# Modulation vectors from TensorE in four 32-column groups, in a hybrid Fourier / RG-LRU / PEER layer

## The chip, the core and the metric

The kernel runs on one core of a Trainium2 chip. The metric is the device time of one launch in microseconds (us). Engines are named as in the profile: PE (TensorE matmul) and PEld (its weight loads), DVE (VectorE), ACT (ScalarE), POOL (GpSimd) and SP (SyncE, which here only issues DMAs).

## The reference

One layer over 512 latent tokens and 256 context tokens of width 1024. Two conditioning vectors, `c` for the latents and `c_ctx` for the context, become six modulation vectors of 1024 each:

```
mod_x = silu(c) @ w_mod + b_mod        # w_mod: 1024 x 6144, fp32, 25 MB
mod_c = silu(c_ctx) @ w_mod + b_mod
sh1, sc1, g1, sh2, sc2, g2 = split(mod, 6)
hx = rmsnorm(x, norm1_g) * (1 + sc1_x) + sh1_x
hc = rmsnorm(ctx, norm1_g) * (1 + sc1_c) + sh1_c
f, u, g = split(h @ w_in, ...)                       # 512 columns each
...                                                  # Fourier group of f; conv, gates and scans of u; gelu(g)
x = x + g1_x * (concat(rmsnorm(fourier), rmsnorm(rec)) @ w_out)
h2 = rmsnorm(x, norm2_g) * (1 + sc2_x) + sh2_x
x = x + g2_x * peer_ffn(h2)                          # product keys, 16384 experts
return rmsnorm(x, final_norm_g)
```

The context needs only the first two of its six vectors, since only its recurrences' last states are used.

## The kernel before

Channels lie on the 128 partitions: x is eight tiles `x2[d]` of 128 x 512, the context eight of 128 x 256, and a modulation vector is eight columns of the tile `mods` (128 x 48) or, for the context, of `modc` (128 x 16: columns 0 to 7 are sh1, 8 to 15 are sc1). Matmuls of full precision are made of three passes in a rounded fp32 form (`mm3`, lines 128 to 130: high x high, high x low, low x high), so each weight tile is split into a high part (ACT copy, `whi`) and a low part (subtraction, `wlo`, line 119, on DVE unless POOL is named). The few matmuls in plain fp32 show as two PE rows each.

The work up to about 300 us is written out by hand; `in_order` pins PE, ACT and DVE to the order of the program text. DMAs on the SP queue follow the pool's buffers: a weight tile of 1 MB (`load`, tile `raw`) can be fetched only when one of the two buffers of its tag is free. The stages, with the lines by which they can be found:

- Start: x, ctx and the first part of `w_mod` are loaded. The sc1 columns are row products: `w_mod` arrives transposed (one output column per partition, 1024 inputs along it), and `mod_dot` (line 229) multiplies a 128 x 1024 block by silu(c), broadcast to all partitions, and sums it on DVE; for the context POOL multiplies (line 239) and ACT sums. The sh1 vectors are matmuls instead (`shift_mm`, line 258: two stationary columns, 512 moving ones, plain fp32), turned into columns by eight tiny matmuls (`shift_cols`, line 264).
- `norm1` multiplies by the reciprocal root mean square on DVE and POOL; `make_hx` scales and shifts on ACT, rounds on ACT, and takes the low part on DVE.
- The projections of u (`u_mm`, `u_block`), convolutions (lines 391 to 395), gates (`gates`), gate branches (`gate_branch`), decays, scans (lines 448 to 455).
- The Fourier projection `f_mm`, the DFT over positions (`dft_seq`) and over head channels (`dft_head`).
- The output projection: eight rounds of `out_mm` (24 passes each), `out_add` (lines 678, 681), the next weights, `rec_norm`; then the sums of squares of the new x (`x2_sums`), their reciprocal root, and `h2` (lines 755 to 757).
- PEER, from about 299 us to the end.

The columns 16 to 47 of `mods` (g1, sh2, sc2, g2) are made by `mod_cols(w)`: it loads 1 MB of `w_mod` and makes two dots of 128 x 1024 on DVE. These calls stand between the steps above: four among gates, branches and scans, three in the Fourier projection, two in the DFT of the heads (as four `mod_col`), and seven in the output projection, one after each round but the last. g1 is needed from the first `out_add`; sh2 and sc2 at `h2`; g2 in PEER.

## Time and profile before

| | |
|---|---|
| median of 3 runs | 1640.66 us (1638.37 to 1642.04) |
| the profiled execution, own time | 1642.68 us |
| its span in the trace | 1640.8 us |
| PE busy, whole span | 1480.7 us (90%) |
| DVE busy, whole span | 1320.9 us (81%) |
| ACT, POOL busy | 641.8 us, 586.1 us |
| granted PE clock, mean | 0.962 of full speed |

How to read it: the part up to 299 us is where the change lies. In the table by stages a row gives the length of a stretch, then the busy time of each engine in it with the number of instructions, the granted PE clock, the DMA engines' busy share and the data rate. In a list in order of time a row gives start, duration, engine, line, operation, tiles and shapes, the count of instructions run together, and in brackets how long the engine sat idle before it and what released it.

### The profile page before, as it was taken

The numbers are of one execution on the slowest core, as the hardware profiler recorded it, in microseconds if no ns is written. First come the engines' busy times: TensorE is split into PE (matmuls) and PEld (weight loads), VectorE is DVE, ScalarE is ACT, GpSimd is POOL, SyncE is SP. The second block draws the span as 40 slices with busy tenths as digits, with TensorE's granted clock in tenths as the row PEclk, the third lists the DMA queues.
The fourth block names the chain that finished last, engine by engine and source line by source line (L and its number), as shares of the span: only waits on it lengthen the run. The fifth ranks groups of instructions, "written<-read, shape, count | busy, mean of one in ns | idle before, by whom it ended". The sixth has DMA issues, their size and how long they took to land.

```text
span 1640.8 us, 22365 instructions
## 1 busy us (share of the span) xinstructions
PE 1480.7 (90%) x8423; PEld 1383.7 (84%) x8423; DVE 1320.9 (81%) x2366; ACT 641.8 (39%) x957; POOL 586.1 (36%) x415
## 2 busy tenths in 40 slices
PE   2896886799989999999899998999999999889986
PEld 0484664588869999999899998999999999889986
DVE  7689989699988996676778787778777778789973
ACT  4656641433334555333242332323323232224342
POOL 6325356466430000323333533334343334322312
PEclk9997898899999999999999999999999999999998
DMA  9223535223216998986879787788878788899831
GB/s 345 99 77 113 181 120 227 92 87 103 94 71 232 295 307 267 360 327 221 314 263 335 284 308 297 261 328 287 320 276 317 275 301 308 294 352 336 301 109 44
DMA packets 125393, 390.92 MB, mean 238 GB/s; under 512 B 9060, under 2 KB 62436, under 8 KB 101988
## 3 DMA queue, kind: packets, MB, share of 16 engines
q1 hardware_dynamic: 88132, 254.93, 43.2%
q0 software_dynamic: 37152, 134.56, 23.0%
q8 instruction: 66, 1.08, 0.3%
q14 instruction: 43, 0.35, 0.1%
HBM read 354.33 MB, written 35.13 MB: 237 GB/s over the span
## 4 chain that ended last, share of the span: by engine, by line
PE 42%; DVE 15%; DMA 14%; issue 12%; POOL 5%; ACT 2%; DVEq 0%; POOLq 0%; SPq 0%; ACTq 0%
PE ps_ps L129 8%; PE ps_ps L128 8%; PE ps_ps L130 8%; DMA row<-vrow,eidx 6%; DMA row<-urow,eidx 6%; PE ps_pa L128 5%; PE ps_pa L130 5%; PE ps_pa L129 5%; POOL row L1068 4%; DVE wlo L119 3%; DVE oacc L1090 1%; PE ps_ps L980 1%; PE ps_ps L981 1%; DVE junk L229 1%; DVE row L1074 1%
## 5 line engine op out<-in xcount | busy, mean ns | idle before, releaser
L66 ACT ACTIVATE whi<-raw 128x1024 fp32r<-128x1024 f32 x296 | 312.7, 1059 | 734.4 <-PE ps_ps L129 398.2
L128 PE MATMUL ps_pa<-h2h,whi 128*128 128x384 f32 x1024 | 354.5, 346 | 15.2 <-ACT act L66 15.2
L129 PE MATMUL ps_ps<-wl,whi 128*128 128x384 f32 x1024 | 349.0, 341 | 7.9 <-DVE wl L119 7.9
L130 PE MATMUL ps_ps<-wh,wlo 128*128 128x384 f32 x1024 | 349.2, 341 | 7.5 <-DVE wlo L119 7.5
L130 PE MATMUL ps_pa<-h2h,wlo 128*128 128x384 f32 x1024 | 350.8, 343 | 5.4 <-DVE wlo L119 5.4
L128 PE MATMUL ps_ps<-wh,whi 128*128 128x384 f32 x1024 | 349.1, 341 | 4.4 <-ACT wh L66 4.1
L129 PE MATMUL ps_pa<-h2l,whi 128*128 128x384 f32 x1024 | 351.6, 343 | 0.0
L119 DVE TENSOR_TENSOR wlo<-raw,whi 128x1024 fp32r<-128x1024 f32 x263 | 325.4, 1239 | 31.8 <-ACT whi L66 29.1
L1068 POOL DMA_INDIRECT row<-urow,eidx x128 | 163.4, 1277 | 447.1 <-DVE row L1074 238.5
L1068 POOL DMA_INDIRECT row<-vrow,eidx x128 | 167.9, 1312 | 292.2 <-DVE oacc L1090 216.6
L1074 DVE SCALAR_TENSOR_TENSOR row<-row,hrow 128x1024 f32<-128x1024 f32 x128 | 155.1, 1221 | 92.2 <-DMA row<-urow,eidx 91.9
L1090 DVE SCALAR_TENSOR_TENSOR oacc<-row,gw,oacc 128x1024 f32<-128x1024 f32 x127 | 162.5, 1279 | 70.9 <-DMA row<-vrow,eidx 70.7
L128 PEld LDWEIGHTS ps_pa<-h2h,whi 128*128 128x128 f32 x1024 | 196.1, 191 | 17.8 <-ACT act L66 16.5
L130 PEld LDWEIGHTS ps_ps<-wh,wlo 128*128 128x128 f32 x1024 | 194.9, 190 | 9.4 <-DVE wlo L119 9.3
L129 PEld LDWEIGHTS ps_ps<-wl,whi 128*128 128x128 f32 x1024 | 194.8, 190 | 8.7 <-DVE wl L119 8.7
L130 PEld LDWEIGHTS ps_pa<-h2h,wlo 128*128 128x128 f32 x1024 | 195.4, 191 | 7.1 <-DVE wlo L119 6.7
L128 PEld LDWEIGHTS ps_ps<-wh,whi 128*128 128x128 f32 x1024 | 194.9, 190 | 4.9 <-ACT wh L66 4.4
L129 PEld LDWEIGHTS ps_pa<-h2l,whi 128*128 128x128 f32 x1024 | 196.0, 191 | 0.5
L119 POOL TENSOR_TENSOR wlo<-raw,whi 128x1024 fp32r<-128x1024 f32 x33 | 80.7, 2446 | 103.2 <-ACT whi L66 70.2
L1039 DVE SCALAR_TENSOR_TENSOR x<-ps_ps,mods,x 128x384 f32<-128x384 f32 x128 | 78.3, 611 | 31.0 <-PE ps_ps L130 30.7
L1014 DVE TENSOR_TENSOR act<-act,gt 128x384 f32<-128x384 f32 x128 | 67.7, 551 | 11.1 <-DMA gt<-Gd 10.1
L66 ACT ACTIVATE wh<-act 128x384 fp32r<-128x384 f32 x128 | 62.7, 518 | 24.1 <-DVE act L1014 21.8
(280 smaller groups left out, 2137.5 us busy)
## 6 DMA issues: line engine op xcount, KB each, us to landing
raw<-u SPq DMA_DIRECT2D x64, 1024.0 KB
raw<-v SPq DMA_DIRECT2D x64, 1024.0 KB
Gd<-stg SPq DMA_DIRECT2D x24, 1024.0 KB
gt<-Gd SPq DMA_DIRECT2D x16, 1536.0 KB
raw<-wm SPq DMA_DIRECT2D x18, 1024.0 KB
raw<-wq SPq DMA_DIRECT2D x8, 1024.0 KB
Ad<-act SPq DMA_DIRECT2D x10, 768.0 KB
act<-Ad SPq DMA_DIRECT2D x10, 768.0 KB
```

Of the source, the lines that this page charges most:

```text
L66: return S.activation(o, i, f, **kw)
L119: lo_ins[0] = (lo_eng or V).tensor_tensor(dst[1], src, dst[0].bitcast(F32), op=ALU.subtract).ins
L128: PE.matmul(ps, a[0], b[0], start=start, stop=False)
L129: PE.matmul(ps, a[0], b[1], start=False, stop=False)
L130: PE.matmul(ps, a[1], b[0], start=False, stop=stop)
L229: return V.scalar_tensor_tensor(junk, wt, 1.0, sil[z], op0=ALU.mult, op1=ALU.mult, accum_out=dst).ins
L980: PE.matmul(o, X0[:, k, :, r], Y1[:, k, :, r], start=True, stop=False)
L1014: V.tensor_tensor(av, av, self.gt[:, :, j], op=ALU.mult)
L1039: V.scalar_tensor_tensor(xd, ps[:, :TD], mods[:, 40 + d:41 + d], xd, op0=ALU.mult, op1=ALU.add)
L1068: G.indirect_dma_start(out=t[:TG], out_offset=None, in_=tab, in_offset=bass.IndirectOffsetOnAxis(ap=eidx[:TG, s:s + 1], axis=0))
L1074: ins = V.scalar_tensor_tensor(t, t, 1.0, hrow[:TG], op0=ALU.mult, op1=ALU.mult, accum_out=dots[:TG, s:s + 1])
L1090: ins = V.scalar_tensor_tensor(o, t, gw[:TG, s:s + 1], o, op0=ALU.mult, op1=ALU.add)
```

## The change

All 48 columns of `mods` and 16 of `modc` come from PE. `w_mod` is kept in natural layout and loaded as 24 tiles of 128 inputs x 2048 outputs (`mod_load(n)`, n = 8m + d: m is the third of the outputs, d the eighth of the inputs). The stationary operand `cc32[:, d]` is 128 x 32: silu(c), silu(c_ctx) and thirty columns of zeros. `mod_mm(n)` makes four plain fp32 matmuls of 512 moving columns; number j writes PSUM partitions 32j to 32j+31, so each uses another 32-column group of the array, and a third is summed over its eight loads in one PSUM bank (`pm`). `mod_out(m)` copies the bank to SBUF on ACT, turns it with four matmuls against a selection matrix (four columns for each vector), and adds the bias on DVE.

```diff
+    cc32 = cpool.tile([P, ND, 32], F32, name="cc32")
+    V.memset(cc32, 0.0)
-    (loads of two broadcast c vectors, of sc1 blocks 0 to 3, of 16 shift tiles; x and ctx between them)
+    def mod_load(n, st=""):
+        rawm[n] = load(wm[n // 8, n % 8], st)
+    for d in range(ND):
+        nc.sync.dma_start(x2[d], xT[d])
+    for n in range(4):
+        mod_load(n, ("", "U")[n % 2])
+    for d in range(ND):
+        nc.sync.dma_start(xn[d][:, :C], ctxT[d])
+    for n in range(4, 8):
+        mod_load(n, ("", "U")[n % 2])
     rawu = {0: load(wu[0], cuts=2)}
...
-    def mod_dot(dst, wt, z): ...      # DVE row product with sum
-    def sc_dots(w): ...               # two dots, two POOL products
-    def shift_mm(n, ds): ...
+    def mod_mm(n):
+        m, d = n // 8, n % 8
+        if d == 0:
+            modp[m] = pst("pm")
+        t = rawm.pop(n)
+        for j in range(4):
+            PE.matmul(modp[m][32 * j:32 * j + 32], cc32[:, d], t[:, j * 512:(j + 1) * 512],
+                      start=(d == 0), stop=(d == ND - 1))
+    def mod_out(m):
+        sb = bt(F32, 512)
+        act(sb, modp[m], AF.Copy)
+        pT = pst("pa", 32)
+        for b in range(4):
+            PE.matmul(pT[:, 8 * b:8 * b + 8], sb[:, b * P:(b + 1) * P], vec[:, V_SEL:V_SEL + 8], start=True, stop=True)
+        ...                             # one bias add into mods, for m = 0 one into modc
...
+    mean_squares(x2, T, ssx, range(ND))
+    for n in range(3):
+        mod_mm(n)
     mean_squares([xn[d][:, sc] for d in range(ND)], C, ssc, range(ND))
+    for n in range(3, 8):
+        mod_mm(n)
+    mod_out(0)
-    (norm1 on DVE and POOL; make_hx: two scale-and-shift and a rounding on ACT, one subtraction on DVE)
+    def hx_norm(d):
+        hx.append(bt2(L))
+        for z, src, sl, mm in ((1, xn[d][:, sc], sc, modc), (0, x2[d], sx, mods)):
+            V.scalar_tensor_tensor(xn[d][:, sl], src, A1[:, z, d:d + 1], rstd[:, sl], op0=ALU.mult, op1=ALU.mult)
+            act(hx[d][0][:, sl], xn[d][:, sl], AF.Identity, bias=mm[:, d:d + 1])
+    def hx_low(d):                      # two DVE operations, 256 and 512 wide
...
     def mod_cols(w, st=""):
-        mod_col(2 * w, st)
-        mod_col(2 * w + 1, st)
+        mod_load(8 + w, st)
+        if w:
+            mod_mm(7 + w)
+        if w == 8:
+            mod_out(1)
...
-    ss2 = pst("pa")                     # and ssf = pst("pm")
+    ss2 = []                            # both taken from "pa" where they are used
...
-    rsqrt(rstd2, bt(F32, 512), ss2, 1024)
-    mod_bias(24, 48)
+    rsqrt(rstd2, bt(F32, 512), ss2[0], 1024)
+    mod_mm(23)
+    mod_out(2)
```

The low part of the second half of the first weights moves from POOL to DVE. The loads of columns 16 to 47 stand where they stood, as many MB, but a block is multiplied one `mod_cols` call later than it is loaded.

On PE at the very start (L282 and L241 are the sums of squares, L258 the shift matmuls, L211 the four-group matmuls, L264 and L219 the turning ones), the rows up to the first projection:

```order
-L282 MATMUL ps_ps<-b,ones 128x512 x4
-L258 MATMUL ps_pa<-b,cc 2x512 x4
-L282 MATMUL ps_ps<-b,ones 128x256 x8
-L258 MATMUL ps_pa<-b,cc 2x512 x4
-L264 MATMUL ps_pm<-i_101,b 128x2 x4
-L258 MATMUL ps_pa<-b,cc 2x512 x4
+L1211 UNCONDITIONAL_BRANCH
+L241 MATMUL ps_ps<-b,ones 128x512 x4
+L211 MATMUL ps_pm<-raw,cc_98 32x512 x12
+L241 MATMUL ps_ps<-b,ones 128x256 x8
+L211 MATMUL ps_pm<-raw,cc_98 32x512 x20
+L219 MATMUL ps_pa<-vec,b 128x8 x4
```

Eight blocks (32 matmuls) now stand ahead of the first projection, split by the context's sums of squares.

On PE between the gates of the last two channel blocks and the last gate branch:

```order
 L129 MATMUL ps_ps<-b,whi 128x512
 L130 MATMUL ps_ps<-b,wlo 128x512
+L211 MATMUL ps_pm<-raw,cc_98 32x512 x12
 L128 MATMUL ps_pa<-b,whi 128x512
 L129 MATMUL ps_pa<-b,whi 128x512
```

Three blocks in a row are put in there; the first frees the buffer of the next Fourier weights.

On DVE in the rounds of the output projection, before (L229 is a dot, L681 an `out_add`, L119 a low part, L609 a `rec_norm` split) and then after (L622, L119 and L552 are the same three):

```order
L229 SCALAR_TENSOR_TENSOR junk,mods<-raw,sil 128x1024 x2
L681 SCALAR_TENSOR_TENSOR b<-ps_ps,mods,b 128x512 x2
L119 TENSOR_TENSOR wlo<-raw,whi 128x1024
L609 SCALAR_TENSOR_TENSOR b<-b,vec 128x512 x2
L229 SCALAR_TENSOR_TENSOR junk,mods<-raw,sil 128x1024 x2
L681 SCALAR_TENSOR_TENSOR b<-ps_ps,mods,b 128x512 x2
```

```order
L622 SCALAR_TENSOR_TENSOR b<-ps_ps,mods,b 128x512 x2
L119 TENSOR_TENSOR wlo<-raw,whi 128x1024
L552 SCALAR_TENSOR_TENSOR b<-b,vec 128x512 x2
L622 SCALAR_TENSOR_TENSOR b<-ps_ps,mods,b 128x512 x2
```

The two dots between rounds are gone from DVE; on PE one block stands after each round's 24 passes instead.

More of the change, by code (lines that the diff above doesn't have):

```diff
@@ L218, in build @@
     tact(sg, cc, AF.Sigmoid)
-    V.tensor_tensor(cc, cc, sg, op=ALU.mult)
-    for z in range(2):
-        for q in range(2):
-            sg = bt(F32, 512)
-            o = sil[z][:, q * 512:(q + 1) * 512]
-            tact(sg, o, AF.Sigmoid)
-            V.tensor_tensor(o, o, sg, op=ALU.mult)
-    def mod_dot(dst, wt, z):
-        junk = p1c.tile([P, 1024], mybir.dt.bfloat16, tag="junk", name="junk")
-        return V.scalar_tensor_tensor(junk, wt, 1.0, sil[z], op0=ALU.mult, op1=ALU.mult, accum_out=dst).ins
@@ L231, in mod_bias @@
-    def mod_bias(a, b):
-        V.tensor_tensor(mods[:, a:b], mods[:, a:b], vec[:, V_BMOD + a:V_BMOD + b], op=ALU.add)
-    def sc_dots(w):
-        for k in (2 * w, 2 * w + 1):
-            mod_dot(mods[:, 8 + k:9 + k], wsc[k], 0)
-            tag = ("whi", "wlo")[k % 2]
-            pr = wspl.tile([P, 1024], F32, tag=tag, name=tag)
-            G.tensor_tensor(pr, wsc[k], sil[1], op=ALU.mult)
-            prods.append((pr, modc[:, 8 + k:9 + k]))
-    prods = []
-    def sc_sums(n):
-        for _ in range(n):
-            pr, dst = prods.pop(0)
-            act(pr, pr, AF.Copy, accum_out=dst)
@@ L250, in build @@
-    shp = [pst("pa"), pst("pa")]
-    shr = [bt(F32, 512), bt(F32, 512)]
-    shT = pst("pm", 16)
-    shv = shT.rearrange("p (d z) -> p z d", z=2)
-    hx = []
-    def shift_mm(n, ds):
-        for d in ds:
-            PE.matmul(shp[n][:2], cc[:, d, :], wsh[d, n], start=(d == 0), stop=(d == ND - 1))
-        if d == ND - 1:
-            act(shr[n][:2], shp[n][:2], AF.Copy)
-    def shift_cols(n):
-        for d in range(4 * n, 4 * n + 4):
-            PE.matmul(shT[:, 2 * d:2 * d + 2], shr[n][:2, d % 4 * P:(d % 4 + 1) * P], i2, start=True, stop=True)
-        sl = slice(4 * n, 4 * n + 4)
-        for z, mm in enumerate((mods, modc)):
-            V.tensor_tensor(mm[:, sl], shv[:, z, sl], vec[:, V_BMOD + 4 * n:V_BMOD + 4 * n + 4], op=ALU.add)
+    V.tensor_tensor(cc32[:, :, 0:2], cc, sg, op=ALU.mult)
@@ L323, in build @@
+    def hx_low(d):
+        for sl, mm in ((sc, modc), (sx, mods)):
+            V.scalar_tensor_tensor(hx[d][1][:, sl], xn[d][:, sl], mm[:, d:d + 1], hx[d][0][:, sl].bitcast(F32),
+                                   op0=ALU.add, op1=ALU.subtract)
     pss0 = [(pst(), pst()) for h in range(2)]
@@ L359, in build @@
     decay = decay_rates()
-    for d in range(4, ND):
-        make_hx(d)
+    for d in range(3, ND):
+        hx_norm(d)
+        hx_low(d - 1)
         next(decay, None)
-    for d in range(2, ND):
-        u_mm(pss0, wpu, d)
+        u_mm(pss0, wpu, d - 1)
+    hx_low(ND - 1)
+    u_mm(pss0, wpu, ND - 1)
+    for _ in decay:
+        pass
     wpu1 = [split_w(rawu[1], h, V, "U") for h in range(2)]
```

123 lines of the change are left out of this document (32 added, 91 removed).

## The prediction

> **What bounds the kernel now.** The change ends at about 299 us, so I first cut the span into the stages of the program and read the busy times of each (length, then PE, PEld, DVE, ACT, POOL, the granted PE clock, DMA share, GB/s):
>
> ```profile
> 0.00:41.00 41.00, 8.20 (x10) 2.35 (x11) 29.31 (x23) 16.57 (x27) 27.64 (x15) 1.00 0.96 345
> 61.20:89.40 28.20, 27.75 (x130) 20.32 (x131) 15.26 (x40) 20.63 (x30) 2.39 (x1) 0.89 0.14 44
> 89.40:134.60 45.20, 39.57 (x200) 32.80 (x198) 37.24 (x52) 28.60 (x42) 18.42 (x8) 0.98 0.23 89
> 134.60:161.90 27.30, 17.16 (x73) 13.86 (x73) 26.58 (x22) 14.96 (x25) 15.30 (x6) 0.75 0.30 116
> 161.90:187.90 26.00, 24.67 (x97) 19.26 (x97) 25.76 (x26) 18.62 (x22) 8.44 (x5) 0.91 0.66 239
> 187.90:203.00 15.10, 8.69 (x48) 8.29 (x48) 15.00 (x16) 8.52 (x12) 4.17 (x2) 0.77 0.22 79
> 203.00:216.10 13.10, 10.78 (x71) 10.22 (x72) 12.07 (x22) 6.08 (x14) 5.04 (x3) 0.87 0.45 160
> 216.10:277.60 61.50, 48.66 (x198) 37.21 (x196) 54.91 (x60) 19.78 (x27) 37.08 (x20) 0.94 0.43 155
> 277.60:299.30 21.70, 5.51 (x7) 1.88 (x7) 15.26 (x20) 5.90 (x9) 11.75 (x6) 0.69 0.46 165
> 299.30:1640.00 1340.70, 1274.90 (x7549) 1231.95 (x7549) 1071.05 (x2068) 491.19 (x731) 444.90 (x343) 0.97 0.72 256
> ```
>
> The reader sees four kinds of stage: the loads fill the first 41 us (DMA share 0.96); PE carries 61 to 130 us; DVE carries 134 to 203 us and most of the output projection; the last 1341 us are PE work that the change does not touch. Next I asked for the dots, by group and then by stretch (dots and the reads of their sums on DVE):
>
> ```profile
> L229 DVE SCALAR_TENSOR_TENSOR junk<-raw,sil 128x1024 bf16<-128x1024 f32 x36 | 67.6, 1878 | 1.9 <-DMA raw<-wm 1.3
> 61.20:134.60 73.40, 4.91 (x8) 0.94 0.20 72
> 134.60:216.10 81.50, 23.27 (x26) 0.83 0.43 155
> 216.10:277.60 61.50, 24.93 (x25) 0.94 0.43 155
> 277.60:299.30 21.70, 3.78 (x6) 0.69 0.46 165
> ```
>
> After the start 56.9 us of DVE go, all of it in stages where DVE is short. What comes back is on PE, and how dear that is decides the case. The nearest rows are the shift matmuls, plain fp32, 512 moving columns, and a tiny one:
>
> ```profile
> 47.66 3.59 PE L258 MATMUL ps_pa<-b,cc 128*2 128x512 f32 x8
> 70.60 0.59 ACT L66 ACTIVATE b<-ps_pa 2x512 f32<-2x512 f32 x1 [2.25 <-PE ps_pa L258]
> 72.79 1.05 PE L264 MATMUL ps_pm<-i,b 2*128 2x2 f32 x8
> ```
>
> Four matmuls are eight PE rows in 3.59 us: an fp32 matmul of 512 columns is two passes of 0.45 us, here with only two stationary columns.
>
> **The price X of one load's block** (four matmuls, eight passes) is shown by no row, since nothing before uses a second column group. Upper bound: nothing overlaps, 3.6 us. Lower bound: all four groups run side by side and only the two passes of a group follow one another, 2 x 0.45 = 0.9 us. Between them: the passes are issued in order, group by group, high then low; a group's second pass needs the same 32 columns as its first and waits, and the next group's first pass, behind it, can only run beside that second one. That is five steps, 2.2 us, and I take it, between the ends because the order of the passes allows no more and no row excludes it. A sum by the upper bound stands beside it everywhere.
>
> The Trainium skill, "TensorE: Matmul & The Clock Gate", Part 3, reports 2.38x for three column groups at 512 columns, which would put X near 1.1 us as an estimate. The same part says that a weight load overlaps running matmuls only when its row group differs; all four groups here span all rows, which speaks against the change and for 3.6 us. "TensorEngine Tiling (Array Packing)", Key Properties, adds that changing the tiling mode drains the array, twice per block. No row here shows any of it.
>
> **The start.** The first projection and the first convolution stand at
>
> ```profile
> 61.24 0.58 PE L128 MATMUL ps_ps<-b,whi 128*128 128x256 f32 x1 [4.74 <-ACT b L66]
> 84.33 0.17 DVE L353 TENSOR_TENSOR sp<-sp,s__180 128x8 f32<-128x8 f32 x1
> 88.25 1.22 DVE L119 TENSOR_TENSOR wlo<-raw,whi 128x1024 fp32r<-128x1024 f32 x1 [0.93 <-ACT whi L66]
> 89.40 0.41 DVE L391 TENSOR_SCALAR b<-pad,vec 128x256 f32<-128x256 f32 x1
> 90.17 0.48 DVE L394 SCALAR_TENSOR_TENSOR b<-pad,vec,b 128x256 f32<-128x256 f32 x1
> 90.57 0.74 DVE L395 SCALAR_TENSOR_TENSOR b<-pad,vec,b 128x512 f32<-128x512 f32 x1
> ```
>
> Between 41 and 61 us before, the loads are there and DVE, POOL and ACT still work off dots, products, sums and norms. Now 2 MB of x, 8 MB of weights and 1 MB of context (11.5 million bytes) at 345 GB/s take 33 us; with the first issues 36 us. Then the last block 2.2, the ACT copy 0.6, the turning matmuls 1.05, four small DVE operations of 0.17: 40.6 us. From there DVE is the chain: per channel tile two operations of 0.48 and two of 0.74, x 8 = 19.5; two low parts of 1.22; 26 decay operations of 0.17 = 4.4; together 26.3, to 66.9. The rounding on ACT that went, and POOL's norms, are off the path; POOL's low part that DVE takes over is in the sum. Three more low parts (3.7) and the evacuation of the first projections (2.5) give a first convolution at 73.1 instead of 89.4 us: **-16.3**. With X = 3.6, PE works off eight blocks (29 us from about 14 us, when the first has landed) and the context's sums between, some 5 us later: **-11**.
>
> **Gates and branches, 89.4 to 134.6.** PE is busy without a gap up to its wait
>
> ```profile
> 134.61 0.58 PE L128 MATMUL ps_ps<-b,whi 128*128 128x256 f32 x1 [4.18 <-ACT whi L66]
> ```
>
> so the 4.9 us of dots saved on DVE buy nothing, and two blocks (4.4) just fill the 4.18: **+0.2**; with 3.6 us, **+3**.
>
> **Waiting for the Fourier weights, 134.6 to 161.9.** The chain runs scans, dots, load, split, matmul:
>
> ```profile
> 156.01 4.75 DMA raw<-wf
> 160.78 1.07 ACT whi L66
> 161.89 0.79 PE L128 MATMUL ps_ps<-whi,b 128*128 128x512 f32 x1 [7.96 <-ACT whi L66]
> 163.95 0.43 PE ps_ps L130
> 167.04 0.23 PE ps_ps L129
> ```
>
> The load waits for a dot to free its buffer. Now a block frees it on PE, ahead of the last branch (24 passes of 0.23, 5.6 us): the load and the ACT part, 4.75 + 1.07, are under the two following blocks and the branch. PE's 7.96 idle us are replaced by three blocks (6.6): **-1.4**; with 3.6 us, **+2.8**. In the projection itself PE starts warm, which saves eight steps of 0.43 - 0.23 = 1.6 us, against one block: **+0.6** (or +2). Up to 203 us DVE has its own work (15.0 of 15.1 us) and no dot: **0**.
>
> **Heads, 203 to 216.1.** PE idles 2.3 us; two blocks (4.4) and the turning of g1 with its ACT copy (1.65), which PE waits out: **+3.8** (or +6.6). DVE loses its four dots, but PE is then the longer.
>
> **Output projection, 216.1 to 277.6.** Before, PE waits here for DVE, which is late with the second half's operand because dots stand between:
>
> ```profile
> 226.10 1.14 PE ps_pm L704 x2
> 255.74 0.80 PE L129 MATMUL ps_ps<-b,whi 128*128 128x512 f32 x1 [7.28 <-DVE b L609]
> 264.16 3.29 DVE L229 SCALAR_TENSOR_TENSOR junk<-raw,sil 128x1024 bf16<-128x1024 f32 x1
> ```
>
> Without them DVE has 54.9 - 24.9 = 30 us of work in 61.5 and is no longer late. PE has 48.7 plus seven blocks; of its 12.8 idle us some 3 stay (the sums at 226.10 come from POOL). 7 x 2.2 - 9.8 = **+5.6**: the gain on DVE is taken back by PE. With 3.6 us it is **+15.4**.
>
> **The second norm, 277.6 to 299.3.** In order of time:
>
> ```profile
> 277.19 0.39 PE L130 MATMUL ps_ps<-b,wlo 128*128 128x512 f32 x1
> 279.25 1.21 DVE L229 SCALAR_TENSOR_TENSOR junk<-raw,sil 128x1024 bf16<-128x1024 f32 x1
> 282.59 1.40 DVE L678 SCALAR_TENSOR_TENSOR x<-ps_ps,mods,x 128x512 f32<-128x512 f32 x2
> 287.41 1.91 PE L693 MATMUL ps_pa<-b,ones 128*128 128x512 f32 x2
> 290.08 0.69 DVE L147 TENSOR_SCALAR b<-ps_pa 128x512 f32<-128x512 f32 x1 [6.10 <-ACT rstd L66]
> 291.54 2.72 DVE L149 TENSOR_TENSOR b<-b,rstd 128x512 f32<-128x512 f32 x1
> 299.27 1.22 PE L128 MATMUL ps_ps<-h2h,whi 128*128 128x512 f32 x2 [9.95 <-ACT h2h L66]
> ```
>
> The last two dots hold up the last update of x from about 279 to 282.6 us. After, the update comes 1.5 us after the last matmul, the sums another 3, the reciprocal root 0.7 + 2.8 to 6.8 (its operations took 0.69 or 2.72). Beside it PE makes the last block, which nothing covers any more if the root is quick: 2.2 us, or twice that at half the clock, copy 0.6, turning 1.05, then two small and two large operations before the first matmul. I take 14 us instead of 21.7: **-7.7**; with 3.6 us, **-6.5**.
>
> **Sum.** -16.3 + 0.2 - 1.4 + 0.6 + 0 + 3.8 + 5.6 - 7.7 = -15.2 us. The profiled execution took 1642.7 us by its own time, 2.0 more than the median of the runs, 1640.7; put on the median, **1625 us**. From here a difference under 0.2% (3.3 us) counts as none, about what a measurement can tell.
>
> **Rivals.**
> 1. The groups do not run side by side (the change then does not do what it says). For it: no row shows two matmuls at once, and the shift matmuls, one after the other, take their full 0.45 us a pass. Sum: -11 + 3 + 2.8 + 2 + 6.6 + 15.4 - 6.5 = +12.3 us, **1653 us, slower**. The place is the output projection, where seven blocks become the longest work. Between the two sums 1.4 us of X cost 27.5, some 20 us for each us, so the sign changes at X near 3.0 us. It is also what the weight-load rule of the skill would give.
> 2. All groups overlap fully, X about 1.2 us with its transitions: -17.5 - 1.8 - 4.4 - 0.4 + 1.7 - 1.4 - 8.5 = -32 us, **1608 us**. Against it: the two passes of a group are issued back to back. The speedup that the skill reports would give about this.
> 3. The start is not quicker by 16 us: the last early load can only be issued when block 3, behind the context's sums, has freed its buffer, and the weights of u follow it on the same queue. If that costs half of the gain, -8 instead of -16.3: **1633 us**. For it: the first 41 us are DMA-full now, and a gap is not made up.
>
> **Chances.** Forecast 0.38, full overlap 0.25, no overlap 0.27, slow start 0.10. Faster: nearly all of the first, second and fourth, 0.72; same 0.06; slower 0.22, from no overlap less the part of it that lands within the bound or below. The range takes in 1608 with a few us for a better start, and 1653: 1604 to 1653. The likeliest case alone is 1615 to 1635.
>
> **What would show it.** Right: the passes of the new matmuls start less than 0.45 us apart on PE, about 2.2 us to a block; the first projection near 44 us instead of 61 (40.6 and the first operations on DVE and ACT); the first convolution near 73; the wait for `wf` gone; DVE with idle time from 216 us on and PE without; the stretch from the last output matmul to the first of PEER near 14 us. Wrong: blocks of 3 us or more; PE rows in the start that wait for `raw<-wm`; a PE wait for ACT or a PSUM bank around the turning matmuls that costs more than 2 us each.

## The result, and the profile after

The changed kernel takes 1594.35 us in the median of 4 runs (1584.53 to 1597.65), the kernel before beside it 1641.35 (1638.37 to 1644.33): a ratio of 0.970, interval 0.966 to 0.975, so 47 us faster where 15 were forecast. 1594 lies below the range. The profiled execution of the changed kernel took 1597.65 us, its span 1595.9.

The same stages as in the prediction, now of the kernel after (length, then PE, PEld, DVE, ACT, POOL, the granted PE clock, DMA share, GB/s):

```profile
0.00:43.30 43.30, 23.84 (x96) 9.72 (x96) 9.46 (x22) 16.14 (x28) 2.34 (x7) 0.84 0.94 359
43.30:72.30 29.00, 24.20 (x113) 18.90 (x114) 25.41 (x61) 14.28 (x22) 0.00 (x0) 0.88 0.22 81
72.30:140.80 68.50, 62.86 (x312) 48.71 (x311) 50.12 (x57) 45.14 (x67) 28.65 (x14) 0.93 0.30 116
140.80:172.40 31.60, 30.20 (x153) 23.96 (x151) 24.41 (x24) 25.34 (x32) 9.38 (x5) 1.00 0.43 158
172.40:190.70 18.30, 13.87 (x97) 10.72 (x98) 12.00 (x20) 7.13 (x16) 6.29 (x4) 0.91 0.40 135
190.70:250.60 59.90, 56.53 (x255) 37.77 (x254) 34.85 (x37) 22.34 (x31) 36.47 (x22) 0.97 0.56 205
250.60:259.90 9.30, 4.93 (x23) 1.86 (x22) 6.11 (x11) 3.80 (x7) 5.30 (x3) 0.91 0.33 125
259.90:1595.00 1335.10, 1271.74 (x7549) 1227.77 (x7549) 1070.16 (x2068) 491.10 (x731) 445.37 (x343) 0.98 0.71 257
```

The reader sees that PE now carries the Fourier projection (30.2 of 31.6 us) and the output projection (56.5 of 59.9), where DVE did before, and that DVE has 34.9 us of work in the output projection instead of 54.9. The loads still fill the start (DMA share 0.94).

In order of time, one block in the output projection between matmuls of the rounds (first fence), and three blocks in a row with their weight loads (second and third):

```profile
210.20 0.39 PE L130 MATMUL ps_ps<-b,wlo 128*128 128x512 f32 x1
210.52 1.06 PE L211 MATMUL ps_pm<-raw,cc 128*32 128x512 f32 x8
211.51 0.50 PE L128 MATMUL ps_ps<-b,whi 128*128 128x512 f32 x1
211.85 0.39 PE L129 MATMUL ps_ps<-b,whi 128*128 128x512 f32 x1
```

```profile
132.53 2.78 PE L211 MATMUL ps_pm<-raw,cc 128*32 128x512 f32 x24
```

```profile
132.53 0.16 PEld L211 LDWEIGHTS ps_pm<-raw,cc 128*32 128x32 f32 x8 [0.36 <-issue]
132.99 0.13 PEld L211 LDWEIGHTS ps_pm<-raw,cc 128*32 128x32 f32 x4 [0.30 <-issue]
133.42 0.13 PEld L211 LDWEIGHTS ps_pm<-raw,cc 128*32 128x32 f32 x4 [0.30 <-issue]
```

Eight passes take 1.06 us and the next matmul starts 0.99 us after the block began; 24 passes take 2.78 us, six steps of 0.43. Behind the first eight, the weight loads come in fours, one for each column group, every 0.43 us. So X is 0.93 to 1.06 us, next to the lower bound. The change from the full array to the groups and back costs something, but little: from the start of the last ordinary matmul ahead of the block (210.20) to the start of the second one behind it (211.85) are 1.65 us, of which 0.86 are the block's two steps and 0.46 two ordinary passes of 0.23. Some 0.3 us are left for the two changes, and a block takes 1.2 us of PE's time in all.

The rest of this document goes by marks on the time axis, read from the time-ordered rows of each kernel's profile (us): the first projection, the first convolution, the first Fourier projection matmul, the first head matmul, the first output matmul, the end of the last one, the first matmul behind the second norm, and what follows to the end of the span.

| kernel | proj. | conv. | Fourier | head | out | out ends | PEER | rest |
|---|---|---|---|---|---|---|---|---|
| before | 61.2 | 89.4 | 161.9 | 199.7 | 216.1 | 277.6 | 299.3 | 1341.5 |
| before, second profile | 60.9 | 89.1 | 161.5 | 199.4 | 215.8 | 277.3 | 298.9 | 1349.5 |
| after | 43.4 | 72.3 | 140.8 | 172.4 | 190.7 | 250.6 | 259.9 | 1336.0 |
| after, second profile | 43.2 | 72.2 | 138.9 | 170.5 | 189.2 | 249.1 | 258.4 | 1340.4 |
| no column groups | 49.3 | 78.2 | 154.6 | 188.4 | 211.5 | 285.5 | 296.3 | 1336.1 |
| two 64-column groups | 41.3 | 70.3 | 142.4 | 174.5 | 194.3 | 258.9 | 268.2 | 1334.6 |
| another order of issue | 42.0 | 71.0 | 137.7 | 169.3 | 187.9 | 247.8 | 257.1 | 1332.8 |
| start only | 44.5 | 73.5 | 146.0 | 183.4 | 200.3 | 262.9 | 283.1 | 1328.5 |
| late part only | 61.1 | 89.2 | 155.9 | 191.0 | 210.1 | 270.0 | 280.2 | 1327.4 |
| after, with row products | 39.6 | 68.5 | 148.8 | 183.7 | 203.1 | 270.3 | 286.8 | 1327.7 |
| decay and split early | 41.7 | 65.6 | 132.4 | 164.0 | 182.3 | 242.3 | 251.5 | 1329.9 |
| old hx | 41.6 | 63.8 | 130.6 | 162.2 | 181.7 | 239.9 | 249.2 | 1332.5 |
| both | 42.3 | 64.5 | 131.2 | 162.8 | 182.3 | 240.5 | 249.9 | 1336.7 |
| old hx, two blocks moved | 42.2 | 65.3 | 132.1 | 163.7 | 180.8 | 237.9 | 247.3 | 1328.6 |

The part up to PEER repeats within 2 us between two profiles of one kernel; the rest does not. From kernel to kernel the start moves more than that: the program up to the first projection is the same in the changed kernel and in the one with row products, and the mark stands at 43.4, 43.2 and 39.6 us. So a gain of less than some 4 us is read below from the length of a stage and not from one mark.

### The profile page after: what moved, and what is told of

It is laid out like the page before. It is cut to its first block, busy times and chain, and to the rows that moved or that the text cites. A ratio compares the mean times of both kernels' runs of the same rounds, so it can differ in the third digit from the quotient of the medians.

```text
span 1595.9 us, 22544 instructions
## 1 busy us (share of the span) xinstructions
PE 1488.2 (93%) x8591; PEld 1379.4 (86%) x8591; DVE 1232.5 (77%) x2296; ACT 625.3 (39%) x930; POOL 533.8 (33%) x398
## 4 chain that ended last, share of the span: by engine, by line
PE 45%; DMA 19%; issue 13%; DVE 13%; POOL 5%; ACT 4%; SPq 0%; DVEq 0%; POOLq 0%; ACTq 0%
DMA row<-vrow,eidx 10%; PE ps_ps L128 7%; PE ps_ps L129 7%; PE ps_ps L130 7%; PE ps_pa L128 6%; PE ps_pa L129 6%; PE ps_pa L130 6%; DMA row<-urow,eidx 6%; POOL row L1012 4%; DVE wlo L119 2%; DVE oacc L1034 2%; PE ps_ps L924 1%; PE ps_ps L925 1%; ACT whi L66 1%; ACT b L66 1%
## 5 line engine op out<-in xcount | busy, mean ns | idle before, releaser
L128 PE MATMUL ps_pa<-h2h,whi 128*128 128x384 f32 x1024 | 353.8, 346 | 11.3 <-ACT act L66 11.3
L119 DVE TENSOR_TENSOR wlo<-raw,whi 128x1024 fp32r<-128x1024 f32 x264 | 326.5, 1239 | 41.4 <-ACT whi L66 38.9
L129 PEld LDWEIGHTS ps_ps<-wl,whi 128*128 128x128 f32 x1024 | 194.3, 190 | 10.8 <-DVE wl L119 10.7
L130 PEld LDWEIGHTS ps_ps<-wh,wlo 128*128 128x128 f32 x1024 | 194.3, 190 | 10.2 <-DVE wlo L119 10.1
L128 PEld LDWEIGHTS ps_ps<-wh,whi 128*128 128x128 f32 x1024 | 194.3, 190 | 3.6 <-ACT wh L66 3.1
L119 POOL TENSOR_TENSOR wlo<-raw,whi 128x1024 fp32r<-128x1024 f32 x32 | 76.6, 2395 | 96.8 <-ACT whi L66 67.8
L983 DVE SCALAR_TENSOR_TENSOR x<-ps_ps,mods,x 128x384 f32<-128x384 f32 x128 | 78.2, 611 | 33.1 <-PE ps_ps L130 33.0
L66 ACT ACTIVATE wh<-act 128x384 fp32r<-128x384 f32 x128 | 62.8, 518 | 25.2 <-DVE act L958 21.8
```

What stands on the lines that cost most here:

```text
L66: return S.activation(o, i, f, **kw)
L119: lo_ins[0] = (lo_eng or V).tensor_tensor(dst[1], src, dst[0].bitcast(F32), op=ALU.subtract).ins
L128: PE.matmul(ps, a[0], b[0], start=start, stop=False)
L129: PE.matmul(ps, a[0], b[1], start=False, stop=False)
L130: PE.matmul(ps, a[1], b[0], start=False, stop=stop)
L983: V.scalar_tensor_tensor(xd, ps[:, :TD], mods[:, 40 + d:41 + d], xd, op0=ALU.mult, op1=ALU.add)
```

## The experiments

Theory: the price X of a block sets the time, X is about 1 us since all four groups run at once, and what DVE lost in row products it lost from its critical chain. Rivals: the price matters little; the order of issue makes the price; the gain lies elsewhere.

**No column groups, and two groups.** The stationary operand becomes wider, with zeros around the two silu columns; number and length of the matmuls stay.

```diff
-            PE.matmul(modp[m][32 * j:32 * j + 32], cc32[:, d], t[:, j * 512:(j + 1) * 512],
-                      start=(d == 0), stop=(d == ND - 1))
+            o = 96 + 128 * d - 32 * j          # window on a strip of zeros, silu every 128 columns
+            PE.matmul(modp[m], strip[:, o:o + 128], t[:, j * 512:(j + 1) * 512],
+                      start=(d == 0 and j == 0), stop=(d == ND - 1 and j == 3))
```

```diff
+        for j in (0, 2, 1, 3):                 # strip: silu every 64 columns
+            g, o = j // 2 * 64, 32 + 64 * d - 32 * (j % 2)
+            PE.matmul(modp[m][g:g + 64], strip[:, o:o + 64], t[:, j * 512:(j + 1) * 512],
+                      start=(d == 0 and j % 2 == 0), stop=(d == ND - 1 and j % 2 == 1))
```

> The changed kernel with the column groups taken away and nothing else: the stationary operand is 128 columns wide, zero but for the two silu columns, which a shifted window puts at column 32j, and the four matmuls of a load accumulate into one full bank of 128 partitions. The same 32 matmuls of 512 columns per third of w_mod, the same loads, the same turning. Theory A (the price X of a load's block sets the time, and it is near 1.0 us only because the four groups run side by side): a block takes 3.4 to 3.6 us, as the eight rows of 3.59 us in the kernel before; by the prediction's slope of about 20 us of time per us of X the kernel takes 1594 + 20 x 2.5 = about 1645 us (1635 to 1655), and most of it is lost between the first output matmul and the last (7 blocks) and in the start (8 blocks). Rival B (the gain is VectorE's and GpSimd's relief, and the blocks lie in TensorE's waits): blocks of 3.5 us, but no more than 1605 us.

> The changed kernel with two 64-column groups instead of four of 32: the stationary operand is 64 wide, two of the four matmuls of a load share a group, issued in the order 0, 2, 1, 3. Theory A: a block takes half of the serial price, 1.75 us, and the time lies between the changed kernel and the serial one on a line: 1594 + 20 x 0.8 = about 1610 us (1605 to 1617). Rival B (relief elsewhere): 1594 to 1598 us. Rival C (any grouping already frees the array, the number of groups does not matter): X stays near 1.0 and the time at 1594.

The groups of the modulation matmuls by line and shape, of the changed kernel, with two groups, and with none (count | PE busy, mean ns of a pass | idle before):

```profile
L211 PE MATMUL ps_pm<-raw,cc 128*32 128x512 f32 x192 | 26.6, 647 | 5.3 <-DMA raw<-wm 5.3
```

```profile
L212 PE MATMUL ps_pm<-raw,strip 128*64 128x512 f32 x192 | 46.8, 620 | 1.1 <-DMA raw<-wm 1.1
```

```profile
L212 PE MATMUL ps_pm<-raw,strip 128*128 128x512 f32 x192 | 86.1, 598 | 0.0
```

Over 24 blocks that is 1.11, 1.95 and 3.59 us a block: the price follows the number of groups. Without groups the cost of the change is gone too:

```profile
231.59 0.40 PE L130 MATMUL ps_ps<-b,wlo 128*128 128x512 f32 x1
231.82 3.60 PE L212 MATMUL ps_pm<-raw,strip 128*128 128x512 f32 x8
235.49 0.39 PE L129 MATMUL ps_ps<-b,whi 128*128 128x512 f32 x1
```

From 231.59 to 235.49, the second ordinary matmul behind the block, are 3.90 us: eight passes of 0.43 and two of 0.23, and nothing left. The times are 1594, 1602.9 (1600.8 to 1604.6; ratio 0.978, 0.975 to 0.980) and 1632.8 us (1625.8 to 1642.8; ratio 0.996, 0.992 to 1.000). Both lie below what the theory expected, 1605 to 1617 and 1635 to 1655. The relief-only rival, which allowed 1605 us, falls, and so does the one by which any grouping would do. To the mark of PEER, where scatter is small, the steps against the second profile of the changed kernel are +9.8 us for 0.84 us of X and +37.9 for 2.48 (+8.3 and +36.4 against the first): 10 to 12 us for each us of X up to 1.95, then 17, not a line of 20. Below about 2 us the eight blocks of the start are hidden by the loads: PE waits 5.3 us for `raw<-wm` with four groups, 1.1 with two, none without groups, where the first projection comes 6 us late. At the full price of 3.6 us the change is still not slower than before. That was the rival the prediction gave 1653 us.

**Another order of issue.** In the start, loads are taken in pairs and two neighbouring matmuls want the same group.

```diff
-        for j in range(4):
-            PE.matmul(modp[m][32 * j:32 * j + 32], cc32[:, d], ...)
+        for j in range(4):
+            for i, n in enumerate(ns):
+                PE.matmul(modp[m][32 * j:32 * j + 32], cc32[:, n % 8], t[i][:, j * 512:(j + 1) * 512], ...)
...
-    for n in range(3):
-        mod_mm(n)
+    mod_mm(0, 1)
+    mod_mm(2)
-    for n in range(3, 8):
-        mod_mm(n)
+    mod_mm(3)
+    mod_mm(4, 5)
+    mod_mm(6, 7)
```

> The changed kernel with the first third's blocks in another order of issue: loads (0, 1), (4, 5) and (6, 7) are taken in pairs, and for each column group the matmul of the first load is followed at once by that of the second, so that two neighbours in the program want the same group. The work is the same. It asks why a block takes two steps (eight passes in 0.86 us) and not the five that the prediction took. Theory E (TensorE takes matmuls strictly in the order of the program, and a matmul that must wait for its group holds up those behind it; the block of the changed kernel takes two steps only because its four neighbours want four groups): the 16 passes of the pair (0, 1), 2.25 us in the changed kernel at that clock, form a staircase of five matmuls of two steps and take about 5 us; the pairs behind the loads 4.3 us. Theory F (each group has a queue of its own and the order does not matter): 2.2 to 2.4 us for the first pair, 1.7 to 1.8 us for the others. The time stays within 5 us of 1594, since loads end last there.

The pair (4, 5): ten passes, block 3 and the first two of the pair, are done when PE stops for load 5. That PE stops there, with load 4 in place and six of its passes still to come, shows that it was given the matmuls in the order of the text. Then the other 14, in time order and in windows of 0.40 to 0.45 us (length, PE busy, passes that run in the window, granted clock, DMA share, GB/s), and their weight loads:

```profile
28.66 1.94 PE L213 MATMUL ps_pm<-raw,cc 128*32 128x512 f32 x14 [1.55 <-DMA raw<-wm]
```

```profile
28.60:29.05 0.45, 0.39 (x4) 1.00 1.12 473
29.05:29.50 0.45, 0.45 (x8) 1.00 0.95 400
29.50:29.90 0.40, 0.40 (x7) 1.00 0.97 410
29.90:30.30 0.40, 0.40 (x6) 1.00 1.12 471
```

```profile
28.66 0.17 PEld L213 LDWEIGHTS ps_pm<-raw,cc 128*32 128x32 f32 x8 [2.46 <-DMA raw<-wm]
29.12 0.14 PEld L213 LDWEIGHTS ps_pm<-raw,cc 128*32 128x32 f32 x3 [0.29 <-issue]
29.55 0.14 PEld L213 LDWEIGHTS ps_pm<-raw,cc 128*32 128x32 f32 x3 [0.29 <-issue]
```

A pass lasts longer than a window, so a window counts those that start in it and those still running: four start, then four, three and three. Group 0 has two passes left, the others four each, and that is what the steps show. In strict order the second matmul of each group would have held up the first one of the group after the next, and the 14 passes would have taken four times 0.86, 3.4 us. They took 1.94. So each group takes its own passes as it becomes free, and a pass that waits for its group does not hold up the other groups. A matmul that waits for a load does: the six passes of load 4 stood behind the first of load 5 and lost 1.55 us with it. The whole took 1591.7 us in one execution.

The Trainium skill, "TensorE: Matmul & The Clock Gate", Part 3, says that matmuls start in strict program order and that a weight load overlaps running matmuls only where its row group differs. These rows disagree with both for column groups: three weight loads are made at 29.12 while four passes run on the same rows. Its 2.38x for three groups agrees with them: 3.59 / 1.11 is 3.2x for four, 3.9x with three blocks in a row.

**The start alone, and the late part alone.**

```diff
     def mod_cols(w, st=""):           # start alone: columns 16 to 47 as before
-        mod_load(8 + w, st)
-        if w:
-            mod_mm(7 + w)
-        if w == 8:
-            mod_out(1)
+        mod_col(2 * w, st)
+        mod_col(2 * w + 1, st)
```

The late part alone is the kernel before with `mod_load`, `mod_mm` and `mod_out` of the change in `mod_cols` and at the second norm.

> Only the start changed: columns 0 to 15 by TensorE in four groups as in the changed kernel, columns 16 to 47 by VectorE's row products from transposed w_mod as in the kernel before, in the same places. Theory A: the first convolution stands at about 72 us instead of 89.4, later stages last as before, the tail from the last output matmul to the first matmul behind the second norm is 21.7 us again: 1641 - 17 = 1624 us. Rival D (the head start is eaten by a wait for loads or for POOL later on): 1635 or more. If start and late part add up, this gain and that of the late part alone give the 46 us of the whole.

> Only the late part changed: the start as in the kernel before (row products, GpSimd products, shift columns by TensorE), columns 16 to 47 by TensorE in four groups. Theory A: the first convolution at 89.4 as before, then waits for the Fourier weights and the Fourier stage shorter by 4 to 10 us together, the output projection no longer (-2 to 0 us), the tail 9 to 10 us instead of 21.7: 1641 - 28 = 1613 us if the 5.5 us that the expert part was shorter belong to the change, 1618 if they are scatter between runs. Rival D (VectorE's relief is worth nothing without the early start): 1630 or more.

Measured: 1616.0 us (1613.3 to 1618.8; ratio 0.986, 0.984 to 0.989) and 1608.0 us (1603.6 to 1609.4; 0.980, 0.978 to 0.983). To the mark of PEER, 16.2 and 19.1 us are won, 35.3 together, against 39.4 to 40.9 for both: nearly additive. (The start alone also loads and makes the broadcast silu(c) that its row products need.) The start's gain is not eaten later on: from the first convolution to PEER it takes 209.6 us, the kernel before 209.9. What is missing lies mostly in the Fourier projection, which takes 37.8 us before, 37.4 with the start alone, 35.1 with the late part alone and 31.6 with both; why it needs both was not tried. The tail (from the end of the last output matmul to PEER) is 20.2 us with row products and 10.2 without, so its gain belongs to the late part. The first time is 8 us below what was expected, the second 5 or 10, and that lies behind the mark, in the rest.

**The change, with DVE loaded as before.** Two row products on DVE come to each late block, into a scrap column that nothing reads.

```diff
             PE.matmul(modp[m][32 * j:32 * j + 32], ...)
+        if m:
+            for b in range(2):
+                V.scalar_tensor_tensor(junk, t[:, b * 1024:(b + 1) * 1024], 1.0, t[:, 0:1024], op0=ALU.mult,
+                                       op1=ALU.mult, accum_out=scrap[:, ...])
```

> The changed kernel with VectorE loaded as before behind the start: to each of the 16 late blocks of TensorE come two row products of 1024 elements on VectorE in the old form, over the same loaded weights, into a scrap column that nothing reads. It asks whether the late gain is VectorE's relief, which the prediction priced at little in the Fourier projection (+0.6 us where -6.2 was measured). Theory J (VectorE's 32 products stood on the chain to the splits and scans, and taking them off is the whole late gain): the Fourier stage is 37 to 38 us again instead of 31.6, the tail 18 to 22 instead of 9.3, the first matmul behind the second norm at 283 to 290 us, the whole 1620 to 1628 us. Rival K (the gain is that loads' buffers come free sooner, or that the new kernel orders its waits otherwise): the Fourier stage stays below 34 us and the whole below 1608.

Measured: 1625.5 us (1616.2 to 1629.9; ratio 0.990, 0.987 to 0.994), and PEER at 286.8 instead of 258.4 to 259.9, with a start that was 4 us earlier. From the first convolution to PEER that is 218.3 us, where the changed kernel has 186.3 to 187.5 and the kernel before 209.9. So the row products cost 31 to 32 us here, more than the late part ever won, and the edit does more than load DVE. It also keeps the buffers: a load now waits for the product that last reads its buffer, as in the kernel before, and PE's blocks, which stand in program order, wait for the load. Below are the longest of these waits, ahead of the second and third of three blocks in a row, then all of PE's waits for `w_mod` from the first convolution to PEER and the DMA queue's waits for the products (the last two as us in total, times, longest):

```profile
139.62 3.64 PE L213 MATMUL ps_pm<-raw,cc 128*32 128x512 f32 x16 [11.64 <-DMA raw<-wm]
```

```profile
PE ps_pm L213 <- DMA raw<-wm: 21.8, 5, 11.6
```

```profile
SPq L111 <- DVE junk L218: 111.8, 15, 18.1
```

The changed kernel and the late part alone have no such wait there. All of it falls into two stages, 14.7 us ahead of the Fourier projection and 7.1 in the output projection, which are 12 to 14 and 7 us longer than in the changed kernel: there the run cannot tell DVE's work from buffers that come free late. It can in the Fourier projection and the tail, where PE waits for no load. The Fourier stage is 34.9 us, 3.3 more than without the products and between the theory's 37 and the rival's bound of 34; the tail is 16.6, 7.3 more, below the theory's 18 to 22. So the products cost some 11 us in these two stages without any wait for loads, and that DVE's relief is the whole late gain is not shown. PEER and the whole time lie in the theory's ranges (283 to 290, 1620 to 1628 us), but most of the way there is PE waiting for loads. DVE in the Fourier stage, with the products and then without them, the first rows of the scan of channel block 2 and what stands ahead of it:

```profile
162.91 1.21 DVE L218 SCALAR_TENSOR_TENSOR junk<-raw 128x1024 bf16<-128x1024 f32 x1
...
164.17 1.23 DVE L218 SCALAR_TENSOR_TENSOR junk<-raw 128x1024 bf16<-128x1024 f32 x1
...
165.32 1.22 DVE L119 TENSOR_TENSOR wlo<-raw,whi 128x1024 fp32r<-128x1024 f32 x1
166.46 0.95 DVE L405 TENSOR_TENSOR b<-b 128x768 f32<-128x768 f32 x1
```

```profile
152.89 0.96 DVE L391 SCALAR_TENSOR_TENSOR b<-b 128x768 f32<-128x768 f32 x1 [1.36 <-POOL b L390]
153.77 1.22 DVE L119 TENSOR_TENSOR wlo<-raw,whi 128x1024 fp32r<-128x1024 f32 x1
155.59 0.96 DVE L398 TENSOR_TENSOR b<-b 128x768 f32<-128x768 f32 x1 [0.60 <-ACT b L66]
```

With the products the scan starts 17.6 us after the first Fourier matmul (148.8), without them 14.8 (140.8), and DVE has idle time ahead of its work. PE's wait for DVE behind these scans is 2.43 us with the products and 0.60 without.

**DVE's chain in the start.** Three kernels: the decay operations and the first weight split moved into DVE's idle time; the old `norm1` and `make_hx` with the new modulation; both.

```diff
     V.tensor_tensor(cc32[:, :, 0:2], cc, sg, op=ALU.mult)
+    decay_rates()                     # all 25 operations here, none between the tiles of hx
...
         act(sb, modp[m], AF.Copy)
+        if m == 0:
+            wpu.append(split_w(rawu[0], 0))
```

```diff
     rsqrt(rstd[:, sx], m[:, sx], ssx, 1024)
+    for d in range(4):
+        norm1(V, d, x2[d], sx)
+        norm1(G, 4 + d, x2[4 + d], sx)
...                                    # the same for the context
-    hx_norm(d), hx_low(d)
+    make_hx(d)                        # two scale-and-shift and a rounding on ACT, one subtraction on DVE
```

> The changed kernel with two pieces of work moved into VectorE's idle time before the modulation vectors exist: the 25 decay operations stand right after the silu instead of between the tiles of hx, and the first half of the first projection weight is rounded and split right after the copy of the modulation sums instead of behind the first tile. Nothing is left out. Theory G (behind the modulation vectors VectorE's order sets the start, and a gain at the first convolution reaches the end): TensorE's waits for hx in the changed kernel, 0.28 + 0.64 + 0.63 + 1.00 us, and the 2.13 us behind its first matmul go; the first convolution at 68 instead of 72.3, the whole 1590 us (1586 to 1592 in the median against 1594). Rival H (the loads that follow set the later stages): the first convolution at 68, and the whole at 1593 to 1596.

> The changed kernel with the way in which hx was made before: rows of x and of the context times the reciprocal root on VectorE and GpSimd (both idle while w_mod is loaded), scale and shift on ScalarE, rounding on ScalarE, one subtraction on VectorE per tile; the modulation vectors still by TensorE in four groups. It asks how much of the gain is the new hx and not the new modulation. Theory G (VectorE's chain behind the modulation vectors sets the start): VectorE has 1 us to a tile instead of 2.4, TensorE's waits go, the first convolution at 69 to 70 instead of 72.3, the whole at 1591. Rival I (the new hx is part of the gain, for ScalarE now has three operations and 2.1 us to a tile): the first convolution at 73 to 75, the whole at 1595 to 1598.

> The moved work of the run before the last and the old way of making hx together, as the version that might beat both kernels. Theory G: VectorE is free of everything but one subtraction per tile between the modulation vectors and the projection, TensorE is the bound from 42 us on (96 matmuls at 0.12 and 0.23 us in turn, 17 us at full clock, more while it comes up from half): first convolution at 66 to 67, the whole at 1587 (1583 to 1590). Rival H: no more than the better of the two alone, or 1593 to 1596.

Measured: 1587.1 us (1577.6 to 1588.6; ratio 0.968, 0.965 to 0.971), 1582.8 (1580.9 to 1590.5; 0.967, 0.964 to 0.970) and 1588.2 (1584.6 to 1588.5; 0.969, 0.966 to 0.971). The first convolution came at 65.6, 63.8 and 64.5 us, in all three earlier than expected. To PEER they save 7, 9 and 8.5 us against the second profile of the changed kernel, the gain at the first convolution reaching the mark each time. The stretch from the first projection to the first convolution, free of the start's scatter, takes 23.9, 22.2 and 22.2 us instead of 29.0. So the new way of making hx, which came with the change, costs 7 us in that stretch against the old one under the same modulation, and some 9 up to PEER. From the first projection to the first convolution, the kernel with the old hx (columns as in the table by stages above, whose second row is the same stretch of the changed kernel):

```profile
41.50:63.80 22.30, 21.81 (x113) 18.84 (x114) 15.92 (x38) 19.99 (x30) 0.00 (x0) 0.90 0.34 126
```

DVE goes from 25.4 of 29.0 us to 15.9 of 22.3, and PE, with the same 113 passes, from 24.2 of 29.0 to 21.8 of 22.3: it hardly waits any more, which is why both moves together give no more than one.

**Two blocks moved into waits.** The old hx, with block 14 ahead of PE's wait for the split in the heads and block 16 ahead of its wait for POOL's sums.

```diff
     f_mm(3, f1)
+    mod_mm(14)
...
         if k == 0:
+            mod_mm(16)
             ssf, ssr = pst("pa"), pst("pa")
```

> The kernel with the old way of making hx and the new modulation (the fastest so far), with two of the late blocks moved into waits of TensorE that the profile shows: one ahead of the wait for VectorE's split of the first Fourier head (3.68 us), one ahead of the wait for GpSimd's sum of squares in the output projection (2.90 us). Theory A (a late block costs its 1.0 us wherever TensorE is the bound and nothing in a wait): the first matmul behind the second norm at 247.2 us instead of 249.2, the whole 2 us shorter, which the times alone can hardly show. Rival: the loads behind these blocks come no earlier and a later wait grows by the same: 249.2.

PEER starts at 247.3 instead of 249.2, the 2 us that were expected; 1583.4 us (1577.8 to 1584.5), ratio 0.963, 0.961 to 0.966. It has the lowest ratio of the kernels, but its interval overlaps that of the one with the old hx alone (0.964 to 0.970). That it is 2 us is in part luck: this execution reached the first convolution 1.5 us later, and from there to PEER it takes 181.9 us instead of 185.4, 3.5 less. Of these, 2.4 are in the heads and 1.1 in the output projection. The wait for the split is 3.68 us as before, so the first block does not lie in it: it stands 12 us ahead of it, in place of a wait of 0.60 us, and what went is its old place right behind the split, where it took 1.87 us at half the clock (granted 0.50). The second block and the sums behind it:

```profile
187.40 1.06 PE L211 MATMUL ps_pm<-raw,cc 128*32 128x512 f32 x8
190.40 1.12 PE L648 MATMUL ps_pa<-b,ones 128*128 128x512 f32 x2 [1.93 <-POOL b L561]
```

The wait for POOL is 1.93 us and not 2.90: the block lies in it.

**Second profiles of both kernels.**

> The changed kernel once more, for a second profile. From its first matmul behind the second norm to the end the first profile has 1336.0 us, the kernel before 1341.5, and the kernels with one part of the change 1327.5 and 1328.5, with the same instructions in all of them. Theory L (scatter of one kernel from execution to execution): this profile has another number than 1336, by 3 us or more, and the part up to the second norm stays at 257 to 260 us. Theory M (something fixed in the program, such as addresses): 1336 again within 1 us.

> The kernel before once more, for a second profile of the part behind the second norm. Theory L (scatter): between 1328 and 1341 us and not 1341.5. Theory M (the part is longer in this kernel by something fixed): 1341.5 again within 1 us. Up to the second norm 299 us as before.

One execution each: 1600.6 and 1650.3 us. The rest is 1340.4 us instead of 1336.0, and 1349.5 instead of 1341.5; the second value is outside what was expected of it, upward. So one kernel's rest moves by 4 to 8 us between two executions. One of PE's waits in the rest, `ps_pa` at line 128 for ACT's `act`, is 15.2 and 18.0 us in total in the two profiles of the kernel before and 11.3 and 13.0 in those of the changed one; nothing here shows why.

Whether the rest is shorter on average with the change stays open: the two profiles of the kernel before have the two highest values of the table, and the median less the mark of PEER is some 1342 us for before and 1328 to 1339 for the others, while the instructions there are the same. 47 us of gain in the medians less 39.4 to 40.9 up to PEER leave some 6 to 8 us for it.

## Why the prediction was wrong

The direction was right, the size wrong by a factor of three. By its own steps:

- **X, taken as 2.2 us, measured 0.93 to 1.11, or 1.2 with the changes to the groups and back.** This is the step that failed first. "The passes are issued in order, group by group, high then low ... and the next group's first pass, behind it, can only run beside that second one" is not so: each group takes its passes on its own, as the other order of issue showed. The lower bound, two passes of a group behind one another, was the true price of the passes. On a line between the kernels with 1.95 and 3.59 us, an estimate, 2.2 us would put PEER at 268.2 + 0.25 x 17 = 272.5 us, some 14 us behind the 258.4 that was measured.
- **Even with X at 2.2, 26.8 us would have been won up to PEER and not 15.2.** The other 11.6 are the stages below, as the kernel with two groups shows them.
- **The start: right.** -16.3 forecast, -17.1 measured; first projection at 43.4 (near 44), first convolution at 72.3 (73.1), DVE the chain between them. That it fits within 1 us is in part luck, since the first projection stood between 39.6 and 44.5 us in the kernels with this start. What was not asked is whether that chain, which the change itself made, could be shorter: the old hx gives 63.8. The sum for X = 3.6 us was right as well, -11 forecast and -11.2 measured without groups. The third rival, a start that loads hold back, did not come: PE does wait 5.3 us there for `raw<-wm`, which the prediction named as a sign of being wrong, and the start is quick all the same.
- **Gates, branches and the wait for the Fourier weights: +0.2 and -1.4 forecast, -4.0 to -5.7 measured.** The wait for `wf` is gone as said; three blocks take 2.8 us and not 6.6.
- **The Fourier projection, +0.6 forecast, -6.2 measured.** A second failed step. I priced PE's view (a warm clock against a block) and took DVE's work as its own, "no dot: 0". But six row products stood on DVE there, and PE's waits inside that stage were for DVE: 4.8 us in four, and one of 0.6 after the change. The granted clock of the stage was 0.85 before and 1.00 after. In the kernel before, two of the products and the scan that they held up:

```profile
178.54 1.21 DVE L229 SCALAR_TENSOR_TENSOR junk<-raw,sil 128x1024 bf16<-128x1024 f32 x1
...
179.80 1.23 DVE L229 SCALAR_TENSOR_TENSOR junk<-raw,sil 128x1024 bf16<-128x1024 f32 x1
...
182.09 0.95 DVE L448 TENSOR_TENSOR b<-b 128x768 f32<-128x768 f32 x1
```

  That scan began 20.2 us into the stage, where the changed kernel's begins 14.8 us into it. How much of the 6.2 us is the products is not settled: putting them back costs 3.3 us, taking them off without the early start gains 2.7.
- **Heads, +3.8 forecast, +1.9 to +2.3 measured.** PE waits out the turning and its copy as said (0.72 us for ACT, 1.06 for the turning); the rest of the difference is X, 1.2 us instead of 2.2 for two blocks.
- **Output projection, +5.6 forecast, -1.5 measured.** The mechanism was right: DVE idle, PE the bound. Seven blocks at 1.2 instead of 2.2 us make 7 us of difference, and 5.6 - 7 = -1.4 is what came. With two groups it is +3.1, with none +12.6 (+15.4 forecast).
- **The second norm, -7.7 forecast, -12.4 measured: 9.3 us and not 14.** The reciprocal root takes its short form, and the last block lies beside it. DVE, PE and POOL of the changed kernel, then POOL and DVE of the one before:

```profile
250.69 0.75 DVE L619 SCALAR_TENSOR_TENSOR x<-ps_ps,mods,x 128x512 f32<-128x512 f32 x1 [1.97 <-PE ps_ps L130]
254.24 0.69 DVE L147 TENSOR_SCALAR b<-ps_pa 128x512 f32<-128x512 f32 x1 [2.79 <-ACT rstd L66]
254.96 1.18 DVE L148 SCALAR_TENSOR_TENSOR b<-b,rstd 128x512 f32<-128x512 f32 x1
256.17 0.69 DVE L149 TENSOR_TENSOR b<-b,rstd 128x512 f32<-128x512 f32 x1
```

```profile
253.41 1.06 PE L211 MATMUL ps_pm<-raw,cc 128*32 128x512 f32 x8
255.25 1.06 PE L219 MATMUL ps_pa<-vec,b 128*128 128x8 f32 x8 [0.78 <-ACT b L66]
259.86 1.22 PE L128 MATMUL ps_ps<-h2h,whi 128*128 128x512 f32 x2 [3.55 <-ACT h2h L66]
```

```profile
250.91 4.68 POOL L119 TENSOR_TENSOR wlo<-raw,whi 128x1024 fp32r<-128x1024 f32 x2 [4.03 <-ACT whi L66]
```

```profile
291.07 5.38 POOL L119 TENSOR_TENSOR wlo<-raw,whi 128x1024 fp32r<-128x1024 f32 x2 [7.29 <-ACT whi L66]
```

```profile
294.29 2.71 DVE L150 SCALAR_TENSOR_TENSOR rstd<-b,rstd 128x512 f32<-128x512 f32 x1
```

  Before, POOL's split of the next weights (291.07 to 296.45) lay over two of the root's operations, and they took 2.72 and 2.71 us; now it ends at 255.59, and the same two take 0.69. The kernel with the row products shows both in one profile, POOL's split and the same two operations:

```profile
275.76 5.10 POOL L119 TENSOR_TENSOR wlo<-raw,whi 128x1024 fp32r<-128x1024 f32 x2 [5.13 <-ACT whi L66]
```

```profile
278.69 2.72 DVE L149 TENSOR_TENSOR b<-b,rstd 128x512 f32<-128x512 f32 x1
281.45 0.69 DVE L150 SCALAR_TENSOR_TENSOR rstd<-b,rstd 128x512 f32<-128x512 f32 x1
```

  The first lies under the split, the second starts behind its end (280.86). In all profiles of these experiments the two take 2.7 us where the split lies over them and 0.69 where it does not; no run moved the split alone. The Trainium skill, "SBUF — State Buffer", section "Who interferes with whom", says that a VectorE instruction with two SBUF inputs contends with a GpSimd instruction that reads SBUF; the rows agree. The sums are also made at the full clock (granted 1.00 from 250.43 to 253.4 us, 0.57 from 286 to 290 before) and no dot holds up the last update.
- **The rest, 0 forecast, about -6 in the medians**, the size of its scatter; open, as said.
- **Rival 2, full overlap, was the case: 1608 us forecast for it.** It had the right mechanism, the right price of 1.2 us and a chance of 0.25. What was left, 14 us, is the Fourier stage, the tail and the rest. Rival 1 had the right price for its case (3.59 us) and the wrong time: 1632.8 and not 1653, in the main for the same three reasons (Fourier projection -4.0 and not +2, second norm -10.9 and not -6.5, some 5 us in the rest).

## What to carry to other kernels

Matmuls with few stationary columns can share the array by column groups at nearly the full factor, and among matmuls whose operands are there the order in the program does not have to be arranged for it; a narrow fp32 product of 192 passes cost 26.6 us of PE in four groups and 86.1 without. When work leaves an engine, walk that engine's chain in every stage that it crosses, also where another engine looks busy: here one stage that was priced from PE alone was 6 us off. A run that puts work back must not bring a new wait with it: the row products put back also held the buffers, and most of what they cost was PE waiting for loads. And when the new work is beside the old order of things, look at the first chain behind it: the best version kept the change's modulation and took back its new normalisation.

## What the runs showed of the hardware

- Two fp32 matmuls for the same column group that stand next to each other in the program do not hold up those behind them for other groups: 14 passes in 1.94 us, four steps.
- A change from the full array to column groups and back costs some 0.3 us a block: 0.1 ahead of it (0.32 us from the last ordinary pass's start to the block's, against 0.23) and 0.2 behind it (the second ordinary matmul 1.33 us after the block began, with two steps of 0.43 and one pass of 0.23 in it). Without groups there is none of it. The Trainium skill, "TensorEngine Tiling (Array Packing)", Key Properties, says that a change of mode drains the array; the runs agree, with some 0.3 us for both changes together.
- The part of the kernel that the change does not touch took 1327.4 to 1349.5 us with the same instructions, and the kernel before alone 1630 to 1650 us over the runs of these experiments. The length of a stage told changes of 2 us apart that the whole time could not.
